# Two heads per store, computed side by side in TensorE's column halves, in a batched q·kᵀ kernel

## The chip, the cores and the metric

The kernel runs on one core of a Trainium2 chip. The metric is the device time of one execution in microseconds (us). The time before the change is the median of three runs, 1060.26 us (1059.48 to 1061.41).

## The reference

For 8 batches of 12 heads, so 96 heads, q and k are 1024 x 64 in float32 and the output is their product for every head, 1024 x 1024 in float32. Nothing is scaled and there is no softmax.

```python
batch, n_heads, seq, head_dim = 8, 12, 1024, 64

def reference(q, k):
    return np.einsum('bhid,bhjd->bhij', q, k).astype(np.float32)
```

The inputs are 50.3 MB, the output 402.7 MB.

## The kernel before

**Blocks.** The 96 heads are cut into blocks of 2, 2, 4, 8 and then 16 heads (`sizes`). q and k of a block are loaded, cast to float16 and transposed, so that the 64 elements of a head lie on partitions and the rows of a head along the free dimension. A block keeps half of its heads on partitions 0 to 63 and the other half on 64 to 127. Two sets of transposed buffers (`qk_sb`) alternate, so the next block is prepared while the present one is multiplied.

**How a block is prepared.** From block 3 on, q and then k of each block are loaded into the same tile `x_sb` (`Block.load`). Each load first waits on its issuing engine, ScalarE (ACT), until the last cast that reads `x_sb` is done (`input_busy`, set in `cast_quads`). GpSimd (POOL) casts a chunk in four instructions, one for each 32 partitions, into one of three `half` tiles (`cast_quads`, L220). VectorE (DVE) transposes the chunk in 32 x 32 squares into `qk_sb` (`transpose_quads`, L239), which frees the `half` tile. A block of 16 heads has 8 chunks of 2048 elements per partition, four for q and four for k. `TURNS` says after the first PSUM region of which head of the present block each of the next block's chunks is put into VectorE's queue. `LOADS` says after which region of which head ScalarE issues the next load. `to_half` puts casts into GpSimd's queue as early as the `half` tiles and the loads allow.

**The multiplication.** `scores` computes one head. PSUM is cut into two regions of 128 x 2048. For each of the four regions of a head, TensorE loads 128 columns of q (64 rows deep) and multiplies them with two stretches of 512 columns of k, twice. ScalarE copies the region to the output tile (L297), and TensorE goes on to the region after next when the copy is done. VectorE copies none of it, except in the first head. A head's output tile is 128 partitions x 8192 float32 values, 32 KB per partition, and there are three such tiles (`o_sb`, a `Ring`). The first copy of a head waits for the store that last read its tile.

**The stores.** When the copies of a head are done, SyncE (SP) issues one store of 4 MB: partition p holds rows 8p to 8p+7 of the head, one run of 32 KB both in the tile and in memory. The last head is split (`scores_split`) so that one of the 16 DMA engines, the one with partitions 16 to 19 and 48 to 51 (`APART`), is spared the rows of one half store.

**Queues.** Loads from block 4 on are issued from ScalarE's queue, in order with its copies. Stores and the first loads are issued from SyncE's queue. Every engine works in the order in which the Python code records its instructions. An instruction that waits holds all those behind it on its engine.

The lines of the wait before a load and of the wait before a copy are these:

```python
eng.wait(events)                       # Block.load: events = input_busy, the last cast out of x_sb
dma = eng.eng.dma_start(out=self.raw[x], in_=src.rearrange("(p r) d -> p (r d)", p=P))

copied = copier.run(lambda: ..., out_free + [done])   # scores: out_free = the store that last read the tile
```

Of the kernel before, what the change touches and what calls it, by code (L numbers as in the profile page):

```python
# [9 lines left out]
P = 128  # L10
# [53 lines left out]
def kernel(  # L64
# [10 lines left out]
    BH = B * H  # L75
    assert D == 64 and NT == 8 and BH >= 32 and BH % 16 == 0

    flat = [x.rearrange("b h s d -> (b h s) d") for x in (q, k)]
    of = out.rearrange("b h i j -> (b h) i j")

    sizes = [2, 2, 4, 8] + [16] * ((BH - 16) // 16)
    PE_BLOCKS, EARLY = 2, 3
    NMAX = max(sizes)
    CHUNK, HALVES = 64 * 32, 3
    TURNS = (3, 4, 5, 6, 10, 11, 12, 13)
    APART = (16, 48)
    LOADS = {0: {}, 1: {}, 2: {1: 3}, 3: {2: 1}}

# [5 lines left out]
    x_sb = pool.tile([P, NMAX * S * D // P], F32, name="x_sb", tag="x")  # L94
    half_sb = [pool.tile([P, CHUNK], F16, name=f"half{i}", tag=f"half{i}") for i in range(HALVES)]
    qk_sb = [
        [pool.tile([P, NMAX * S // 2], F16, name=f"{'qk'[x]}T{i}") for x in range(2)]
        for i in range(2)
    ]
    o_sb = [pool.tile([P, NT, S], F32, name=f"o_sb{i}", tag=f"out{i}") for i in range(3)]  # L100
    rest_q = pool.tile([P, 64], F16, name="rest_q", tag="rest_q")
# [38 lines left out]
    input_busy = []  # L140
    outs = Ring(o_sb)
    input_landing = [Landing(nc, f"x{i}_in") for i in range(2)]
    tail_landing = Landing(nc, "tail_out")
    rest_landing = Landing(nc, "rest_out")
    store_landing = {id(t): Landing(nc, f"out{i}_out") for i, t in enumerate(o_sb)}

    class Block:
        def __init__(self, i, first, N):
            self.i, self.first, self.N = i, first, N
            self.by_pe = i < PE_BLOCKS  # L150
            self.R = N * S // P
            self.elems = self.R * D
            self.cut = max(1, -(-self.R * 32 // CHUNK))
            self.raw = [None] * 2
            self.landed = [[] for _ in range(2)]
            self.rows = [None] * 2
            self.halves = {}
            self.qk = qk_sb[i % 2]
            self.ready = []
            self.over = []  # L160
# [104 lines left out]
        def scores(self, n, side, regions, w):  # L265
# [48 lines left out]
            out_busy.append(store_landing[id(buf)].start(dma))  # L314

        def scores_split(self, n, regions, w):
            half, g = divmod(n, self.N // 2)
# [138 lines left out]

    early, _, early_busy = outs.next()
    raw = early.rearrange("p t j -> p (t j)")
    at = 0
# [17 lines left out]
    def next_load(eng):  # L477
        if stream:
            b, x = stream.pop(0)
            earlier = (b.i, 0) if x else (b.i - 1, 1)  # L480
            assert b.i == EARLY or not any((i, c[0]) == earlier for i, c in casts)
            b.load(x, eng)
# [32 lines left out]
    def transposed(b, s):  # L515
        b.transpose_quads(*s)
        to_half(b.i)

    def block(i, heads, regions, w):
        b = blocks[i]  # L520
        nxt = blocks[i + 1] if i + 1 < len(blocks) else None
        for n in heads:
            side = {}
            if nxt and nxt.by_pe:
# [9 lines left out]
            elif nxt:  # L534
                parts = nxt.chunks()
                at = TURNS if i > EARLY else [m * b.N // len(parts) for m in range(len(parts))]
                some = [s for m, s in zip(at, parts) if m == n]
                side = {0: [lambda s=s: transposed(nxt, s) for s in some]}
            at = LOADS.get(i, {1: 1, 7: 1})
            if n in at:  # L540
                side[at[n]] = side.get(at[n], []) + [lambda: next_load(act)]
            if i == len(blocks) - 1 and n == b.N - 1:
                b.scores_split(n, regions, w)
            else:
                b.scores(n, side, regions, w)
            to_half(i + 2 + (n == b.N - 1))

# [49 lines left out]
```

## Time and profile before

The profiled execution took 1060.67 us, of which 1058.9 are the span of the profile.

| what | value |
|---|---|
| median of three runs | 1060.26 us (1059.48 to 1061.41) |
| profiled execution, its span | 1060.67 us, 1058.9 us |
| bytes read and written | 50.33 MB and 402.78 MB, 428 GB/s over the span |
| busy, share of the span: TensorE, ScalarE, VectorE, GpSimd | 66%, 66%, 41%, 34% |
| stores of 4 MB (L310) | 95 |
| loads of 4 MB from ScalarE's queue | 10 |

How to read it: the page gives for each engine its busy time, and for the 16 DMA engines the mean share of time in which they had a packet, in 40 slices of 26.5 us. A row of the groups gives the line of the kernel, engine, operation, output and input tiles with partitions x elements, how many there were, busy time, the mean duration of one in nanoseconds, and the idle time of the engine before them with what ended most of it. A packet in the DMA records is one row of a transfer here, that is what one partition holds.

### The profile page before, as it was taken

The page shows a single profiled execution, that of the slowest core. Times are in us where ns is not written, and L with a number is a line of the kernel's source. Part 1 is how long each engine was busy: PE and PEld are TensorE (multiplying, and loading weights), DVE is VectorE, ACT ScalarE, POOL GpSimd, SP SyncE. Part 2 cuts the span into 40 slices and gives each one's busy share as a digit, 9 for nine tenths or more (in the row PEclk, how much of TensorE's full clock was granted, in tenths as well). Part 3 has the DMA queues.
Part 4 walks back from the last instruction along what each step waited for, and adds up shares of the span by engine and source line. Part 5 has one row for each costly group of instructions (what it writes and reads, how often), then busy time and mean ns, then how long its engine had stood idle before and what let it go on. Part 6 is the DMA issues. An engine that isn't in the chain of part 4 may idle for free.

```text
span 1058.9 us, 3350 instructions
## 1 busy us (share of the span) xinstructions
PE 702.3 (66%) x1572; PEld 127.4 (12%) x802; DVE 435.4 (41%) x57; ACT 695.6 (66%) x385; POOL 358.3 (34%) x223
## 2 busy tenths in 40 slices
PE   6875754857477747657765756775674777787771
PEld 1111100111011101101110111110110111111110
DVE  2995939029194008539002917600580930000001
ACT  4766755857477748567765856775674777777771
POOL 7926555056280019065005609100822900000000
DMA  9999999999999999999999999999999999999998
GB/s 378 434 424 433 435 431 434 420 423 428 434 431 433 436 417 435 432 433 433 435 418 436 436 427 430 433 436 429 430 428 428 436 434 434 432 429 433 434 431 366
DMA packets 17186, 453.21 MB, mean 428 GB/s; under 512 B 1929, under 2 KB 1929, under 8 KB 2953
## 3 DMA queue, kind: packets, MB, share of 16 engines
q1 hardware_dynamic: 15008, 408.03, 89.5%
q10 hardware_dynamic: 2016, 42.99, 9.8%
q0 software_dynamic: 144, 1.97, 0.4%
q8 instruction: 9, 0.15, 0.0%
q14 instruction: 9, 0.07, 0.0%
HBM read 50.33 MB, written 402.78 MB: 428 GB/s over the span
## 4 chain that ended last, share of the span: by engine, by line
DMA 65%; ACT 15%; PE 8%; DVE 6%; POOL 4%; issue 1%; SPq 0%; ACTq 0%
DMA out_dram<-o_sb 60%; ACT o_sb L297 15%; PE ps_all L439 7%; DVE kT L239 4%; POOL half L220 3%; DMA x_sb<-in_q_dram 2%; DMA x_sb<-in_k_dram 2%; DVE qT L239 1%; DMA o_sb<-in_q_dram 0%; DVE x_sb L345 0%; DVE o_sb L345 0%; PE ps_all L253 0%; POOL qT L191 0%; DVE kT L260 0%; ACT kT L260 0%
## 5 line engine op out<-in xcount | busy, mean ns | idle before, releaser
L439 PE MATMUL ps_all<-kT,qT 64*128 64x512 f16 x1536 | 696.4, 617 | 327.1 <-ACT o_sb L297 310.0
L297 ACT COPY o_sb<-ps_all 128x2048 f32<-128x2048 f32 (+1 forms) x380 | 687.7, 1859 | 331.6 <-DMA out_dram<-o_sb 286.3
L220 POOL CAST half<-x_sb 32x2048 f16<-32x2048 f32 x176 | 332.5, 1889 | 482.7 <-DMA x_sb<-in_q_dram 307.9
L239 DVE STREAM_TRANSPOSE qT<-half 128x2048 f16<-128x2048 f16 x22 | 202.5, 9477 | 274.0 <-POOL half L220 274.0
L239 DVE STREAM_TRANSPOSE kT<-half 128x2048 f16<-128x2048 f16 x22 | 202.4, 9536 | 132.6 <-POOL half L220 132.6
L436 PEld LDWEIGHTS <-qT 64*128 64x128 f16 x768 | 124.0, 162 | 896.3 <-issue 875.9
L345 DVE COPY x_sb<-ps_all 128x2048 f32<-128x2048 f32 x1 | 2.3, 2292 | 174.0 <-PE ps_all L439 174.0
L374 POOL DMA_INDIRECT out_dram<-x_sb,place x1 | 1.2, 1157 | 176.6 <-DVE x_sb L345 176.6
L239 DVE STREAM_TRANSPOSE kT<-kT 128x1024 f16<-128x1024 f16 x2 | 9.3, 4856 | 0.0
L239 DVE STREAM_TRANSPOSE qT<-qT 128x1024 f16<-128x1024 f16 x2 | 9.2, 4782 | 0.0
L220 POOL CAST qT<-o_sb 32x1024 f16<-32x1024 f32 x8 | 8.3, 1036 | 1.1 <-DMA o_sb<-in_q_dram 0.7
L220 POOL CAST kT<-o_sb 32x1024 f16<-32x1024 f32 x8 | 8.3, 1036 | 0.5
L260 DVE COPY qT<-ps_all 128x1024 f16<-128x1024 f16 x2 | 2.4, 1224 | 11.4 <-PE ps_all L253 11.4
L253 PE MATMUL ps_all<-ident,qT 128*128 128x128 f16 x16 | 2.1, 311 | 7.1 <-POOL qT L191 7.0
L297 DVE COPY o_sb<-ps_all 128x1024 f32<-128x1024 f32 x4 | 4.9, 1225 | 4.4 <-PE ps_all L439 4.4
L345 ACT COPY x_sb<-ps_all 128x2048 f32<-128x2048 f32 (+1 forms) x2 | 3.7, 1860 | 2.1 <-PE ps_all L439 2.1
L260 ACT COPY kT<-ps_all 128x1024 f16<-128x1024 f16 x1 | 1.0, 1013 | 5.1 <-PE ps_all L253 5.1
L366 POOL COPY rest_q<-qT 64x8 f16<-64x8 f16 x4 | 0.6, 197 | 9.9 <-DVE kT L239 9.9
L345 DVE COPY o_sb<-ps_all 128x2048 f32<-128x2048 f32 x1 | 2.3, 2292 | 3.7 <-PE ps_all L439 3.7
L191 POOL CAST qT<-o_sb 128x512 f16<-128x512 f32 x4 | 2.3, 614 | 4.0 <-DMA o_sb<-in_q_dram 4.0
L260 ACT ACT_TABLE_LOAD x1 | 1.3, 1283 | 2.8 <-issue 2.8
L260 DVE COPY kT<-ps_all 128x1024 f16<-128x1024 f16 x1 | 1.2, 1225 | 4.4 <-PE ps_all L253 4.4
(18 smaller groups left out, 14.5 us busy)
## 6 DMA issues: line engine op xcount, KB each, us to landing
out_dram<-o_sb SPq DMA_DIRECT2D x95, 4096.0 KB, 21.8
x_sb<-in_q_dram ACTq DMA_DIRECT2D x5, 4096.0 KB, 25.2
x_sb<-in_k_dram ACTq DMA_DIRECT2D x5, 4096.0 KB, 23.4
x_sb<-in_q_dram SPq DMA_DIRECT2D x1, 2048.0 KB, 14.5
x_sb<-in_k_dram SPq DMA_DIRECT2D x1, 2048.0 KB, 18.9
out_dram<-o_sb SPq DMA_DIRECT2D x1, 2048.0 KB, 17.4
o_sb<-in_k_dram ACTq DMA_DIRECT2D x4, 256.0 KB, 5.2
o_sb<-in_q_dram SPq DMA_DIRECT2D x4, 256.0 KB, 5.4
```

The source lines that it names most:

```text
L191: lambda: nc.gpsimd.tensor_copy(out=rows[:, :, h], in_=self.raw[x][:, h * n : (h + 1) * n].rearrange("p (r d) -> p r d", d=D),),
L220: lambda: nc.gpsimd.tensor_copy(out=dst[q0 : q0 + 32].rearrange("p (r d) -> p r d", d=32), in_=raw[32 * b : 32 * b + 32, c * m : (c + 1) * ...
L239: lambda: nc.vector.transpose(out=dst, in_=buf.rearrange("p (r i) -> p r i", i=32)),
L253: lambda: nc.tensor.transpose(t_ps[:, t], rows[:, t], ident),
L260: lambda: copy(out=dst, in_=t_ps.rearrange("c t m -> c m t")), [done]
L297: lambda: (nc.vector.tensor_copy if by_dve else nc.scalar.copy)(out=dst, in_=ps[:, : w * S]),
L345: lambda: (nc.vector.tensor_copy if copier is dve else nc.scalar.copy)(out=dst[:, t * S : (t + w) * S], in_=ps[:parts, : w * S]),
L366: lambda: nc.gpsimd.tensor_copy(out=packed[:, t, 0, :, c], in_=rows[:, t, :, c]),
L374: nc.gpsimd.indirect_dma_start(out=out.rearrange("b h (m t) j -> (b h m) (t j)", t=T), out_offset=bass.IndirectOffsetOnAxis(ap=place_sb, a ...
L436: return nc.tensor.ldweights(stationary, tile_position=(at, to))
L439: return nc.tensor.add_instruction(mybir.InstMatmult(name=nc.get_next_instruction_name(), ins=[nc.tensor.lower_ap(moving), nc.tensor.lower ...
```

## The change

From head 8 on, two neighbouring heads are computed together (`scores_pair`) and stored with one store of 8 MB. Partition p holds rows 16p to 16p+15 of the two heads taken as one list of 2048 rows, so partitions 0 to 63 hold the first head and 64 to 127 the second, and a partition's run is 64 KB. For that, each of TensorE's instructions takes 64 columns of q instead of 128, and the two heads' instructions alternate: the first head's go to the array's columns 0 to 63 and the second's to columns 64 to 127. A region of PSUM now takes four weight loads and eight matmuls of 64 x 64 x 512 instead of two and four of 64 x 128 x 512, and a pair of heads has eight regions.

The output tiles are one tile of four 32 KB slots. Heads 0 to 7 and the last two use slots singly, the pairs use two neighbouring slots, so there are two pair buffers. To make room, blocks have 2, 2, 4, 6, 10 and then 12 heads, so `x_sb`, the `half` tiles and the transposed tiles are smaller. A load of a block of 12 has 24 KB per partition (3 MB). Chunks are 24 x 32, 20 x 32 and 32 x 32 elements per partition, 12 for a block of 12 heads and 16 for the block of 10.

In a pair VectorE copies regions 3 and 6 and ScalarE the other six; `HELP` lists the pairs in which VectorE takes only region 3, or none. `TURNS` now names head and region after which a chunk's transpose is put into VectorE's queue, `LOADS` the same for the loads in ScalarE's.

```diff
--- before.py
+++ after.py
@@ -73,18 +73,33 @@
     B, H, S, D = q.shape
     NT = S // P
     BH = B * H
-    assert D == 64 and NT == 8 and BH >= 32 and BH % 16 == 0
+    assert D == 64 and NT == 8 and BH >= 36 and BH % 12 == 0
 
     flat = [x.rearrange("b h s d -> (b h s) d") for x in (q, k)]
     of = out.rearrange("b h i j -> (b h) i j")
 
-    sizes = [2, 2, 4, 8] + [16] * ((BH - 16) // 16)
+    sizes = [2, 2, 4, 6, 10] + [12] * (BH // 12 - 2)
     PE_BLOCKS, EARLY = 2, 3
     NMAX = max(sizes)
-    CHUNK, HALVES = 64 * 32, 3
-    TURNS = (3, 4, 5, 6, 10, 11, 12, 13)
+    ROWS, HALVES = 32, 3
     APART = (16, 48)
-    LOADS = {0: {}, 1: {}, 2: {1: 3}, 3: {2: 1}}
+    PAIRS = 3
+    TURNS = {
+        1: [(n, 0) for n in range(2) for _ in range(2)],
+        2: [(n, 0) for n in range(4) for _ in range(2)],
+        3: [(0, 0)] * 8 + [(2, 7)] * 8,
+        4: [(0, 7)] * 2 + [(2, 4)] + [(2, 7)] * 3 + [(6, 7)] * 2 + [(8, 4)] + [(8, 7)] * 3,
+        5: [(0, 7)] * 2 + [(2, 4)] + [(2, 7)] * 3 + [(6, 7)] * 2 + [(8, 4)] + [(8, 7)] * 3,
+    }
+    LOADS = {
+        0: [],
+        1: [],
+        2: [(2, 3)],
+        3: [(2, 0), (4, 7)],
+        4: [(4, 0), (8, 7)],
+        5: [(4, 0), (10, 1)],
+    }
+    HELP = {3: {0: (), 2: (), 4: ()}, 4: {2: (3,), 8: (3,)}, 5: {2: (3,), 8: (3,)}}
 
     pool = ctx.enter_context(tc.tile_pool(name="sb", bufs=1))
     psum = ctx.enter_context(
@@ -92,12 +107,14 @@
     )
     ident = pool.tile([P, P], F16, tag="ident")
     x_sb = pool.tile([P, NMAX * S * D // P], F32, name="x_sb", tag="x")
-    half_sb = [pool.tile([P, CHUNK], F16, name=f"half{i}", tag=f"half{i}") for i in range(HALVES)]
+    half_sb = [pool.tile([P, ROWS * 32], F16, name=f"half{i}", tag=f"half{i}") for i in range(HALVES)]
     qk_sb = [
         [pool.tile([P, NMAX * S // 2], F16, name=f"{'qk'[x]}T{i}") for x in range(2)]
         for i in range(2)
     ]
-    o_sb = [pool.tile([P, NT, S], F32, name=f"o_sb{i}", tag=f"out{i}") for i in range(3)]
+    o_sb = pool.tile([P, 4 * NT, S], F32, name="o_sb", tag="out")
+    slots = [o_sb[:, i * NT : (i + 1) * NT] for i in (2, 3, 0, 1)]
+    doubles = [o_sb[:, 2 * NT :], o_sb[:, : 2 * NT]]
     rest_q = pool.tile([P, 64], F16, name="rest_q", tag="rest_q")
     place_sb = pool.tile([P, 1], I32, name="place", tag="place")
     place_f = pool.tile([P, 1], F32, name="place_f", tag="place_f")
@@ -138,11 +155,12 @@
         ]
     )
     input_busy = []
-    outs = Ring(o_sb)
+    outs = Ring(slots)
+    pairs = Ring(doubles)
     input_landing = [Landing(nc, f"x{i}_in") for i in range(2)]
     tail_landing = Landing(nc, "tail_out")
     rest_landing = Landing(nc, "rest_out")
-    store_landing = {id(t): Landing(nc, f"out{i}_out") for i, t in enumerate(o_sb)}
+    store_landing = {id(t): Landing(nc, f"out{i}_out") for i, t in enumerate(slots + doubles)}
 
     class Block:
         def __init__(self, i, first, N):
@@ -150,7 +168,7 @@
             self.by_pe = i < PE_BLOCKS
             self.R = N * S // P
             self.elems = self.R * D
-            self.cut = max(1, -(-self.R * 32 // CHUNK))
+            self.cut = next(c for c in range(1, self.R) if self.R % c == 0 and self.R // c <= ROWS)
             self.raw = [None] * 2
             self.landed = [[] for _ in range(2)]
             self.rows = [None] * 2
@@ -313,6 +331,62 @@
             )
             out_busy.append(store_landing[id(buf)].start(dma))
 
+        def scores_pair(self, n, side, regions, w, help):
+            qT = self.qk[0].rearrange("c (g m t) -> c g t m", t=2 * NT, m=D)
+            kT = self.qk[1].rearrange("c (g j) -> c g j", j=S)
+            where = [divmod(n + k, self.N // 2) for k in range(2)]
+            buf, out_free, out_busy = pairs.next()
+            written = {}
+            for u in range(2 * NT // w):
+                ps, ps_free, ps_busy = regions.next()
+                for tt in range(w):
+                    stationary = [
+                        qT[half * D : (half + 1) * D, g, w * u + tt] for half, g in where
+                    ]
+                    for k, (half, g) in enumerate(where):
+                        pe.run(
+                            lambda: load_weights(stationary[k], half * D, k * D),
+                            self.ready if n == 0 and u == 0 else [],
+                            signal=False,
+                        )
+                    for j in range(2):
+                        at = tt * S + j * 512
+                        for k, (half, g) in enumerate(where):
+                            moving = kT[half * D : (half + 1) * D, g, j * 512 : (j + 1) * 512]
+                            done = pe.run(
+                                lambda: multiply(
+                                    ps[k * D : (k + 1) * D, at : at + 512],
+                                    stationary[k],
+                                    moving,
+                                    half * D,
+                                    k * D,
+                                ),
+                                ps_free,
+                                signal=tt == w - 1 and j == 1 and k == 1,
+                            )
+                dst = buf[:, w * u : w * u + w].rearrange("p t j -> p (t j)")
+                copier = dve if u in help else act
+                copied = copier.run(
+                    lambda: (nc.vector.tensor_copy if u in help else nc.scalar.copy)(
+                        out=dst, in_=ps
+                    ),
+                    out_free + [done],
+                )
+                written[copier] = copied
+                ps_busy.append(copied)
+                for do in side.get(u, []):
+                    do()
+            self.over = [done]
+            sp.wait(written.values())
+            first = self.first + n
+            dma = nc.sync.dma_start(
+                out=of[first : first + 2]
+                .rearrange("h i j -> (h i) j")
+                .rearrange("(p t) j -> p (t j)", p=P),
+                in_=buf.rearrange("p t j -> p (t j)"),
+            )
+            out_busy.append(store_landing[id(buf)].start(dma))
+
         def scores_split(self, n, regions, w):
             half, g = divmod(n, self.N // 2)
             cs = slice(half * D, (half + 1) * D)
@@ -454,8 +528,8 @@
         blocks.append(Block(i, first, N))
         first += N
 
-    early, _, early_busy = outs.next()
-    raw = early.rearrange("p t j -> p (t j)")
+    early_busy = outs.busy[2]
+    raw = slots[2].rearrange("p t j -> p (t j)")
     at = 0
     for b in blocks[:EARLY]:
         for x in range(2):
@@ -519,7 +593,17 @@
     def block(i, heads, regions, w):
         b = blocks[i]
         nxt = blocks[i + 1] if i + 1 < len(blocks) else None
+        last = i == len(blocks) - 1
+        singles = range(b.N - 2, b.N) if last else range(b.N if i < PAIRS else 0)
+        at = lambda table: table.get(i, table[max(table)])
         for n in heads:
+            if n % 2 and n not in singles:
+                continue
+            if (i, n) == (PAIRS, 0):
+                pairs.busy = [outs.busy[m] + outs.busy[m + 1] for m in (0, 2)]
+            if last and n == b.N - 2:
+                outs.bufs, outs.n = slots[2:], 0
+                outs.busy = [list(pairs.busy[1]) for _ in range(2)]
             side = {}
             if nxt and nxt.by_pe:
                 if n == 1:
@@ -532,18 +616,19 @@
                         for u in (1, 3)
                     }
             elif nxt:
-                parts = nxt.chunks()
-                at = TURNS if i > EARLY else [m * b.N // len(parts) for m in range(len(parts))]
-                some = [s for m, s in zip(at, parts) if m == n]
-                side = {0: [lambda s=s: transposed(nxt, s) for s in some]}
-            at = LOADS.get(i, {1: 1, 7: 1})
-            if n in at:
-                side[at[n]] = side.get(at[n], []) + [lambda: next_load(act)]
-            if i == len(blocks) - 1 and n == b.N - 1:
+                for (m, u), c in zip(at(TURNS), nxt.chunks(), strict=True):
+                    if m == n:
+                        side.setdefault(u, []).append(lambda c=c: transposed(nxt, c))
+            for m, u in at(LOADS):
+                if m == n:
+                    side.setdefault(u, []).append(lambda: (next_load(act), to_half(i + 2)))
+            if last and n == b.N - 1:
                 b.scores_split(n, regions, w)
+            elif n in singles:
+                b.scores(n, side, regions, w)
             else:
-                b.scores(n, side, regions, w)
-            to_half(i + 2 + (n == b.N - 1))
+                b.scores_pair(n, side, regions, w, at(HELP).get(n, (3, 6)))
+            to_half(i + 2 + (n >= b.N - 2))
 
     for b in blocks[:PE_BLOCKS]:
         for x in range(2):
```

## The prediction

> **What bounds the kernel now.** I read the page first (slices, groups, DMA issues), then the chain of waits, the waits by engine, and the packet records.
>
> ```profile
> span 1058.9 us, 3350 instructions
> ...
> DMA  9999999999999999999999999999999999999998
> ...
> L297 ACT COPY o_sb<-ps_all 128x2048 f32<-128x2048 f32 (+1 forms) x380 | 687.7, 1859 | 331.6 <-DMA out_dram<-o_sb 286.3
> L220 POOL CAST half<-x_sb 32x2048 f16<-32x2048 f32 x176 | 332.5, 1889 | 482.7 <-DMA x_sb<-in_q_dram 307.9
> ...
> L345 DVE COPY x_sb<-ps_all 128x2048 f32<-128x2048 f32 x1 | 2.3, 2292 | 174.0 <-PE ps_all L439 174.0
> ...
> L220 POOL CAST qT<-o_sb 32x1024 f16<-32x1024 f32 x8 | 8.3, 1036 | 1.1 <-DMA o_sb<-in_q_dram 0.7
> ...
> x_sb<-in_q_dram ACTq DMA_DIRECT2D x5, 4096.0 KB, 25.2
> x_sb<-in_k_dram ACTq DMA_DIRECT2D x5, 4096.0 KB, 23.4
> ```
>
> The DMA engines never rest: from the first rows to the last few us all 16 have a packet. ScalarE waits 286.3 us for stores to free tiles; no engine but DMA is on the path after the start. So the time is bytes over rate plus any gap in the DMA queue, and each edit is judged by two questions: does it change the rate, and does it open a gap?
>
> The packet records give the rate. A row of 16,384 B takes 611 ns, one of 32,768 B 1,213 ns, so a row costs about 9 ns besides its bytes. Start to start on one engine it is 1,209 ns against 1,204.6 by the slope, so at least 4.6 ns. Stretches without loads run at 433.1 GB/s. The load stretches lose 4.3 us in all, which I leave as it is.
>
> The chain of waits shows what a gap would come from:
>
> ```profile
> 63.83 24.64 DMA x_sb<-in_q_dram
> ...
> 119.69 23.23 DMA x_sb<-in_k_dram
> ```
>
> A load takes 24 us though its own bytes are 9.7 us of DMA time. In the records the first row of the q load starts 3.84 us after its issue (1.0 to reach the engines, as for the kernel's first load, then up to three store rows already taken in), and then its rows start 2.42 us apart on each engine: one load row, one store row. Near the end 16 KB rows start 1.82 us apart beside 32 KB stores, so they alternate row for row whatever their size. In this kernel that is hidden: q and k of a block need 2 x (24 + 16 x 1.95 casts) = 110 us and a block of 16 heads lasts 175.
>
> **The change, part by part.**
>
> *Rows.* 43 pair stores replace 86 stores. Per engine 43 x 8 rows and 43 completions go: 43 x (8 x 4.6 + 6 ns) = 1.8 us, or 43 x 9 x 9 = 3.5 us by the longer reading. Four more loads take back 0.2. I take -1.6.
>
> *TensorE.* Eight matmuls in a row took 3.63 us, so 0.43 each. Two column halves at once are nowhere in this trace. Bounds: at once, a region stays at 4 x 0.43 + 0.2 = 1.9 us; one after the other it is 3.6 us. I take the first, since nothing couples the halves but the order of issue. A pair then takes eight regions at 1.95, 15.7 us from its first copy, plus 0.57 (last packet of the freeing store to the copy) and 1.0 (issue to first row): 17.3 of the 19.4 us of the other pair's store. That hides it with 2 us to spare, where three single tiles had about 10. The Trainium skill (TensorE: Matmul & The Clock Gate, Measured speedup vs the span model) gives 2.38x for three column tiles, 0.79 of ideal; an estimate from it is 2.2 us a region, which makes a pair 17.5 us instead of 15.7, and the sum about 5 us more.
>
> *ScalarE and VectorE.* Six copies of 1.87 and two of 2.29 per pair fit. But VectorE's copies now stand in its queue behind transposes, which wait for casts, which wait for loads. Behind the copy stand the region's release, ScalarE's next copies and the store.
>
> *Loads.* Beside 64 KB rows (2.41 us) a 24 KB row (0.91) takes 3.32, so a load takes 1.0 + 3 x 2.41 + 8 x 3.32 + 0.6 = 35 us when stores are queued. Casts of a q or k of 12 heads: 24 x (1.036 + 0.06) = 26.3; of 10 heads: 32 of 640 elements x 0.78 = 24.9 (0.83 ns per element and 0.18, from the two cast rows). Load and casts cannot overlap, since each load waits for the last cast out of the one `x_sb`. Per block 2 x (35 + 26.3) = 123 us against a block of 6 x 19.4 + 2 x 7.2 = 131. It fits, but hardly, and in the short blocks the chain starts behind:
>
> - q of block 4 is issued after head 6's last copy (71.8), lands at 92.9 (8 x 1.97 beside 32 KB rows), casts to 117.6.
> - k of block 4 then goes; ScalarE has stood at it since about 106, holding the second pair. That pair is stored at 131.2, the DMA queue (8.4 MB pair and 2.6 MB load) ends about 130. **Gap A: 1.0.**
> - k casts to 155.8; q of block 5 lands when the store of heads 12 and 13 is through, 178.4. Heads 14 and 15 follow to 197.9.
> - Heads 16 and 17: region 3 is VectorE's, behind two transposes of q of block 5. Landing 178.4 + 0.6 + first chunk's casts 4.4 + two transposes 8.9 = 192.3; copy 2.3, next region 1.9, three ScalarE copies 5.7: issued at 202.2, rows from 203.2. **Gap B: 5.3.**
> - q of block 5 is cast by 205.3, k lands 35 later, is cast at 267.4, q of block 6 lands at 295.8 behind the store of heads 22 and 23; heads 24 and 25 go out until 315.3. Heads 26 and 27 wait in the same way: 295.8 + 0.6 + 4.4 + 8.9 + 9.9 + 1.0 = 320.6. **Gap C: 5.3.**
> - From block 7 on q is issued at its place in ScalarE's queue (head 10, region 1), about 35 us before it is needed: no gap, no slack.
>
> *Skew.* One engine is slower: the last stores land every 9.76 us (ScalarE goes on at 1002.53, 1012.29, 1022.04), the mean rate makes 9.69. The end spares that engine eight rows of 16 KB, 4.9 us. With 2 us to spare in place of 10 the other 15 cannot run ahead; they idle some 3.6 us and end last, where before the slow one ended about 1.6 after them. I take +2 (bounds 0 and 4).
>
> Sum: -1.6 + 1.0 + 5.3 + 5.3 + 2 = +12.0, on the profiled execution's own 1060.67 (1.8 around its span) 1072.7. The median lies 0.4 lower, so I say **1072** (own range 1066 to 1079: each gap may be 2 us off, skew 2).
>
> **Rivals.**
>
> *Loads come in time (other side).* If beside 64 KB rows a load gets through by bytes or several rows at a turn, q of block 5 lands by 173 and q of block 6 by 290; that is the point from which gaps B and C are gone. Then the rows' saving is left: 1060.3 - 1.6 = 1058.7, at 3.5 saved 1056.8; about 1058. For it: nothing here shows 64 KB rows. Against: row for row at 32 and 16 KB. The Trainium skill (DMA: Bandwidth & Descriptors, Queues, rings and completion order) says that an engine drains a whole packet, typically 9 to 17 descriptors, from one ring before it turns to the next; by that the eight rows of a load would pass together, and this would be the result. The trace shows one row at a turn. Chance 0.27.
>
> *Every block late.* If a load is 3 us longer than 35 (a fourth row taken in ahead, 2.4, or weight loads that show), each of the last four blocks loses up to that: 4 x 2 to 3 more, 1080 to 1084. Chance 0.10.
>
> *It doesn't do what it says: 64 KB is moved as two rows of 32 KB.* The saving shrinks to 0.3, but loads take 1.0 + 3.6 + 8 x 2.12 + 0.6 = 22 to 24 us, gap C goes: 1060.3 - 0.3 + 1 + 5 + 2 = 1068. Chance 0.06.
>
> *TensorE becomes the bound.* Halves one after the other: 8 x 3.6 = 28.9 us a pair against 19.4, 43 x 9.5 = 409 less what loads cover and what the gaps were, 12 x 7.2 and 12: about 1060 + 310 at most, some 1310 where the start hides part. For it: only that no row shows them at once. Chance 0.05.
>
> **How the numbers follow.** Forecast 0.52, rivals 0.27, 0.10, 0.06, 0.05. What can be told from no change is 0.2%, 2.1 us: 1058.1 to 1062.4. The first rival splits on it, 0.18 faster (more than 2.1 saved, between the two readings of the rows) and 0.09 within; the forecast with its gaps nearly filled adds 0.02 within. Faster 0.18, same 0.11, slower 0.71. The range takes in the first rival and the forecast's upper edge: 1057 to 1081 leaves out TensorE, the worst of the late blocks and the best of the first rival, together under 0.2.
>
> **What would show it.** Right: DMA slices below 9 or a dip in GB/s to about 350 near 188 to 214 and 295 to 320; 24 KB loads landing 34 to 36 us after issue; VectorE's copies waiting behind transposes that GpSimd releases; store rows of 64 KB at about 2,417 ns; regions at 1.9 us. Wrong: loads of 24 us with no dip (first rival), rows of 1,213 ns in the pair stores (third), TensorE near 100% (fourth), dips once per block to the end (second). The forecast fails first if the q loads land earlier than I count, for 5 us early removes a gap whole.

## The result, and the profile after

The changed kernel takes 1092.57 us (median of 4 runs, 1091.73 to 1093.83), the kernel before 1060.38 beside it: a ratio of 1.0304, interval 1.0286 to 1.0322. It is slower, as forecast, but by 32 us where 12 were forecast. The span of the profiled execution is 1092.0 us. These are the page's lines of the changed kernel: the span, the 40 slices, two groups of copies, and the loads.

```profile
span 1092.0 us, 5673 instructions
...
PEclk9999655655555555555555555555555555555555
DMA  9999998899979999999999999999999999999998
GB/s 384 441 415 441 428 425 349 374 432 423 420 310 422 431 434 440 423 422 423 404 441 401 443 425 412 429 402 434 432 398 440 405 431 404 389 421 422 437 442 353
...
L370 ACT COPY o_sb<-ps_all 128x2048 f32<-128x2048 f32 x278 | 512.2, 1868 | 457.2 <-PE ps_all L513 246.6
...
L370 DVE COPY o_sb<-ps_all 128x2048 f32<-128x2048 f32 x66 | 154.4, 2340 | 346.5 <-PE ps_all L513 346.5
...
x_sb<-in_q_dram ACTq DMA_DIRECT2D x6, 3072.0 KB, 30.7
x_sb<-in_k_dram ACTq DMA_DIRECT2D x6, 3072.0 KB, 31.8
```

Three things are to be seen. The DMA row has slices of 8 and 7 where it had none but the last. The rate has its deep dips there (349, 374, 310), but it also dips to about 400 once or twice per block to the end, in slices whose DMA digit is 9. And ScalarE, whose longest wait was 286.3 us for stores before, now waits 246.6 us for TensorE, and still 201.6 us for stores.

A DMA digit of 9 says only that packets were under way, so I split the loss by the packet records of the two profiled executions. *Idle* is the time in which fewer than 16 packets were under way, each missing one counted as a sixteenth. *Longer packets* is what the rows took over the median of rows of their size (32 KB 1213 ns, 64 KB 2418, 24 KB 912), summed and divided by 16 engines.

| us | before | after |
|---|---|---|
| longer packets | 5.8 | 14.7 |
| all packets' time, per engine | 1057.2 | 1063.5 |
| idle at 176.4 to 181.8 | 0 | 4.7 |
| idle at 201.1 to 204.5 | 0 | 3.2 |
| idle at 297.2 to 300.3 | 0 | 2.6 |
| idle at 319.6 to 325.7 | 0 | 5.9 |
| idle from block 6 on, eight stretches up to 861 | 0 | 4.4 |
| idle at 908 to 953, the end of block 9 and what follows | 0 | 4.9 |
| idle at the very end | 1.9 | 1.4 |

Packets +6.3 and idle +25.2 make 31.5 of the 33.0 us between the last packets of the two kernels. Packets took 6.3 more although 64 KB rows are nominally shorter than two of 32 KB (2418 against 2426 ns, 2.8 us in all): the excess grew by 8.9.

The dips at 201 and 320 are the two that the prediction described. This is part of the chain of waits of the changed kernel (start us, duration us, what), from the landing of q of block 5:

```profile
160.36 18.62 DMA x_sb<-in_q_dram
178.97 0.05 issue
179.03 1.03 POOL half L238
...
183.37 4.41 DVE qT L257
187.78 0.49 issue
188.27 5.52 DVE qT L257
193.78 2.12 DVE o_sb L370
```

The load lands, GpSimd casts a chunk, VectorE transposes two chunks, and only then copies region 3 of heads 16 and 17. ScalarE waits 7.28 us before its next copy, and the store comes late.

The dips at 176.4 and 297.2 begin at the start of a block. This is ScalarE's timeline in the changed kernel (start, duration, what, and in brackets the idle time before with its releaser):

```profile
115.44 0.33 ACTq L189 DMA_DIRECT2D x_sb<-in_k_dram  x1
115.82 3.63 ACT L370 COPY o_sb<-ps_all 128x2048 f32<-128x2048 f32 x2 [8.04 <-POOL half L238]
...
160.36 0.33 ACTq L189 DMA_DIRECT2D x_sb<-in_q_dram  x1
165.28 3.63 ACT L370 COPY o_sb<-ps_all 128x2048 f32<-128x2048 f32 x2 [20.84 <-PE ps_all L513]
...
283.81 3.63 ACT L370 COPY o_sb<-ps_all 128x2048 f32<-128x2048 f32 x2 [14.98 <-PE ps_all L513]
```

At 165.28 and 283.81 the first pairs of blocks 4 and 5 begin. TensorE had waited for the last transposes of k: 20.7 us ahead of the one, 14.9 ahead of the other. A pair here takes 15.5 us from its first copy to the end of its last, and the rows of its store start about 1 us later, at 181.7 and 300.2. The queue had run dry at 176.4 and 297.2. In block 4 VectorE copies nothing ahead of these transposes. In block 5 it does, as its timeline shows:

```profile
244.56 10.40 DVE L257 STREAM_TRANSPOSE kT<-half 128x1024 f16<-128x1024 f16 x2
258.89 2.29 DVE L370 COPY o_sb<-ps_all 128x2048 f32<-128x2048 f32 x1 [3.93 <-PE ps_all L513]
261.10 20.64 DVE L257 STREAM_TRANSPOSE kT<-half 128x1024 f16<-128x1024 f16 x4
```

The last four transposes stand behind a copy that waits for TensorE. So this dip belongs to VectorE's copies as well, which e12 bears out.

### The profile page after: what moved, and what is told of

Read it like the earlier page. It is cut to its first block, busy times and chain, and to the rows that moved or that the text cites. A ratio compares the mean times of both kernels' runs of the same rounds, so it can differ in the third digit from the quotient of the medians.

```text
span 1092.0 us, 5673 instructions
## 1 busy us (share of the span) xinstructions
PE 694.1 (64%) x2948; PEld 166.3 (15%) x1490; DVE 626.2 (57%) x175; ACT 582.3 (53%) x319; POOL 395.6 (36%) x431
## 4 chain that ended last, share of the span: by engine, by line
DMA 41%; DVE 27%; PE 11%; ACT 8%; POOL 5%; issue 4%; SPq 0%; ACTq 0%
DMA out_dram<-o_sb 33%; DVE qT L257 13%; PE ps_all L513 11%; DVE kT L257 9%; ACT o_sb L370 7%; DMA x_sb<-in_q_dram 6%; POOL half L238 5%; DVE o_sb L370 5%; ACT o_sb L315 2%; DMA x_sb<-in_k_dram 2%; DMA o_sb<-in_q_dram 0%; DVE x_sb L419 0%; DVE o_sb L419 0%; PE ps_all L271 0%; POOL qT L209 0%
## 5 line engine op out<-in xcount | busy, mean ns | idle before, releaser
L513 PE MATMUL ps_all<-kT,qT 64*64 64x512 f16 (+1 forms) x2912 | 688.1, 612 | 365.6 <-ACT o_sb L370 238.3
L370 ACT COPY o_sb<-ps_all 128x2048 f32<-128x2048 f32 x278 | 512.2, 1868 | 457.2 <-PE ps_all L513 246.6
L238 POOL CAST half<-x_sb 32x1024 f16<-32x1024 f32 (+2 forms) x384 | 369.8, 963 | 532.7 <-DMA x_sb<-in_k_dram 220.6
L370 DVE COPY o_sb<-ps_all 128x2048 f32<-128x2048 f32 x66 | 154.4, 2340 | 346.5 <-PE ps_all L513 346.5
L510 PEld LDWEIGHTS <-qT 64*64 64x64 f16 (+1 forms) x1456 | 162.9, 212 | 887.6 <-issue 842.2
L257 DVE STREAM_TRANSPOSE qT<-half 128x1024 f16<-128x1024 f16 (+2 forms) x48 | 224.3, 4901 | 30.8 <-POOL half L238 30.7
L257 DVE STREAM_TRANSPOSE kT<-half 128x1024 f16<-128x1024 f16 (+2 forms) x48 | 224.2, 4906 | 21.9 <-POOL half L238 21.9
L315 ACT COPY o_sb<-ps_all 128x2048 f32<-128x2048 f32 (+1 forms) x36 | 62.2, 1773 | 18.0 <-PE ps_all L513 14.2
L419 DVE COPY o_sb<-ps_all 128x2048 f32<-128x2048 f32 x1 | 2.3, 2292 | 3.7 <-PE ps_all L513 3.7
(20 smaller groups left out, 16.4 us busy)
## 6 DMA issues: line engine op xcount, KB each, us to landing
out_dram<-o_sb SPq DMA_DIRECT2D x9, 4096.0 KB, 15.5
x_sb<-in_q_dram ACTq DMA_DIRECT2D x6, 3072.0 KB, 30.7
x_sb<-in_k_dram ACTq DMA_DIRECT2D x6, 3072.0 KB, 31.8
x_sb<-in_k_dram SPq DMA_DIRECT2D x1, 1536.0 KB, 16.4
```

Source lines behind the costliest of these rows:

```text
L238: lambda: nc.gpsimd.tensor_copy(out=dst[q0 : q0 + 32].rearrange("p (r d) -> p r d", d=32), in_=raw[32 * b : 32 * b + 32, c * m : (c + 1) * ...
L257: lambda: nc.vector.transpose(out=dst, in_=buf.rearrange("p (r i) -> p r i", i=32)),
L315: lambda: (nc.vector.tensor_copy if by_dve else nc.scalar.copy)(out=dst, in_=ps[:, : w * S]),
L370: lambda: (nc.vector.tensor_copy if u in help else nc.scalar.copy)(out=dst, in_=ps),
L419: lambda: (nc.vector.tensor_copy if copier is dve else nc.scalar.copy)(out=dst[:, t * S : (t + w) * S], in_=ps[:parts, : w * S]),
L510: return nc.tensor.ldweights(stationary, tile_position=(at, to))
```

## The experiments

Each line of the table gives the median of the timed runs and the split as above (stretches under 0.1 us left out). The last column is the ratio to the kernel before on the same chip, with its interval.

| kernel | us | longer packets | idle before 400 | idle from 400 on | idle at the end | ratio |
|---|---|---|---|---|---|---|
| changed | 1092.6 | 14.7 | 16.4 | 9.3 | 1.4 | 1.0304 (1.0286 to 1.0322) |
| e12: no copies by VectorE in blocks 4, 5 | 1084.1 | 16.3 | 5.9 | 9.3 | 1.6 | 1.0221 (1.0199 to 1.0243) |
| e1: none at all | 1076.9 | 18.7 | 2.3 | 2.1 | 3.7 | 1.0154 (1.0131 to 1.0178) |
| e5: e1 with 32 KB rows | 1069.4 | 11.6 | 2.5 | 0.3 | 1.0 | 1.0083 (1.0066 to 1.0100) |
| e9: e5, halves stored at once | 1062.6 | 6.4 | 0 | 0.1 | 1.4 | 1.0021 (1.0011 to 1.0031) |
| e4: heads singly, blocks of 12 | 1061.6 | 6.6 | 0 | 0 | 2.6 | 1.0007 (0.9997 to 1.0017) |
| before | 1060.4 | 5.8 | 0 | 0 | 1.9 | |

From the changed kernel over e12, e1, e5 and e9 to the kernel before, the steps are 8.5, 7.2, 7.5, 6.7 and 2.3 us. They add up to the whole 32.2 us, as steps from one end to the other must; what each step shows is in its section. The split is that of one profiled execution each.

### e1: no copies by VectorE

```diff
-    HELP = {3: {0: (), 2: (), 4: ()}, 4: {2: (3,), 8: (3,)}, 5: {2: (3,), 8: (3,)}}
+    HELP = {3: {}}
...
-                b.scores_pair(n, side, regions, w, at(HELP).get(n, (3, 6)))
+                b.scores_pair(n, side, regions, w, at(HELP).get(n, ()))
```

> Edit: ScalarE copies all eight regions of every pair, VectorE none; all else as in the changed kernel (1092.6). Theory (VectorE's copies stand behind transposes in its queue, so late or slow transposes hold back a store): without copies in that queue the dips at 180 to 220 and 300 to 340 and the one that recurs twice per block go, and ScalarE's eight copies of 1.87 fit in 19.4 us: 1060 (1058 to 1065). Rival 1 (two pair buffers leave too little time whoever copies): nothing is gained, 1088 or more. Rival 2 (the chain of load, cast and transpose of a 12-head block is itself longer than the block): TensorE waits at block starts in place of VectorE's copies, 1075 to 1090.

1076.9: half of what the theory promised. The page of this kernel, slices:

```profile
DMA  9999999999999999999999999999999999999998
GB/s 385 431 437 438 415 453 403 422 400 428 431 430 395 442 394 446 408 440 427 401 424 438 417 429 407 447 404 418 429 417 437 415 414 430 432 427 434 427 437 356
```

All deep dips are gone, idle time fell from 27.1 to 8.1 us, and the kernel still loses 16.5 us on the kernel before: the rate falls to about 400 wherever a load runs. So VectorE's copies were one cause, worth 15.7 us. Of the rest, 10.2 us are time in packets (1067.4 per engine against 1057.2), which is no wait of an engine, and 6.2 are idle time. Rival 1 falls as it was put (nothing gained); the time left over is of the kind that it named, and e5 to e11 take it apart. The time lies in the range of rival 2 (1075 to 1090), but its mechanism does not show: TensorE's waits for k's transposes at block starts fell from 38.6 to 31.2 us in all, and in e4 they are 37.8 us and cost nothing.

### e2: the sixth transpose later

```diff
-        5: [(0, 7)] * 2 + [(2, 4)] + [(2, 7)] * 3 + [(6, 7)] * 2 + [(8, 4)] + [(8, 7)] * 3,
+        5: [(0, 7)] * 2 + [(2, 4)] + [(2, 7)] * 2 + [(4, 7)] + [(6, 7)] * 2 + [(8, 4)] + [(8, 7)] * 2 + [(10, 4)],
```

> Edit: in blocks of 12 the sixth transpose of q is recorded after region 7 of the next pair, the sixth of k after region 4 of the next pair, so no more than three transposes stand between two copies of VectorE. Theory: three of 5.2 us and the copy are 18 us, under the 19.4 of a pair, so the dip that recurs twice per block from 440 on goes (about 1.4 us each, eleven of them, 15 us) and the two early dips stay: 1077 (1073 to 1081). Rival 1 (two pair buffers too tight): 1090 or more. Rival 2 (chain longer than the block): 1090 or more, with the last transpose later still.

1090.6 (1088.1 to 1091.3): a miss, 2.0 us gained where 15 were expected, at the time that both rivals gave. I had taken the recurring dips in GB/s for idle time of 1.4 us each. Most of that was longer packets. As e1 had gained 15.7 us with the same two buffers, and e4 shows the chain of the blocks to be short enough, neither rival explains it as put. Four transposes in a row do hold a copy back, as VectorE's timeline of the changed kernel shows at the end of block 9:

```profile
919.18 2.29 DVE L370 COPY o_sb<-ps_all 128x2048 f32<-128x2048 f32 x1 [1.67 <-PE ps_all L513]
921.39 20.66 DVE L257 STREAM_TRANSPOSE kT<-half 128x1024 f16<-128x1024 f16 x4
941.61 2.56 DVE L370 COPY o_sb<-ps_all 128x2048 f32<-128x2048 f32 x1
```

From copy to copy it is 22.4 us, and a pair has 19.4. Here no load follows any more, and it costs 3.0 us of idle time at 949.4. In the blocks before, the same three lines stand beside a load whose rows (7.3 us of DMA time) fill the queue meanwhile. In e2 the idle time at 908 to 953 shrinks from 4.9 to 0.4, the dips before block 6 stay (16.5).

### e3: the output step of the transposes

```diff
+            if self.N == 12:
+                at, side = divmod(part * self.cut + c, 2)
+                dst = self.qk[x][:, at * 2048 : (at + 1) * 2048].rearrange(
+                    "c (i r) -> c r i", i=32
+                )[:, side * m : (side + 1) * m]
...
```

> Edit: the transposes of the 12-head blocks write with a step of 64 elements between a square's columns in place of 96, each chunk to its own place; the output is wrong for these heads, the amount of work is the same. Theory (the price of a transpose follows the step): one takes 4.4 to 4.8 us in place of 5.45, four in a row 18 in place of 20.7, so most of the recurring dip goes: 1078 (1074 to 1083). Rival 3 (VectorE is slowed by GpSimd's casts beside it, not by the step): 5.4 us each and 1092 as before.

1088.0, a miss. Transposes of 1024 elements, in the changed kernel (step 96):

```profile
L257 DVE STREAM_TRANSPOSE kT<-half 128x1024 f16<-128x1024 f16 x36 | 186.3, 5458 | 0.0
```

and in e3 (step 64):

```profile
L263 DVE STREAM_TRANSPOSE kT<-half 128x1024 f16<-128x1024 f16 x36 | 167.5, 4958 | 0.0
```

So the step alone, with the same casts beside it, moves the price by 0.50 us, 9%, and rival 3 falls. In the kernel before (step 128) 2048 elements took 9.5 us, 4.75 for 1024. The time followed by less than expected, 4.6 us, which fits what e2 showed: four in a row are late mostly where a load covers it.

### e4: heads singly

```diff
-    PAIRS = 3
+    PAIRS = 99
...
+                    if m + u // 4 == n:
+                        side.setdefault(u % 4, []).append(lambda c=c: transposed(nxt, c))
...
```

> Edit: every head stored singly (32 KB per partition) from four slots, copied by ScalarE alone, with the blocks of 12, the chunks, the loads and the transposes where the changed kernel has them. Theory: the new blocks cost nothing by themselves, only the pairs with VectorE's copies do: 1061 (1059 to 1064). Rival 2 (the chain of a 12-head block is too long): 1072 or more, with TensorE waiting at block starts.

1061.6, the ratio 1.0007 (0.9997 to 1.0017) can't be told from 1. The blocks of 12, the smaller chunks, the slow transposes and four more loads cost nothing that shows, and the loads land in 22.0 us. TensorE waits 37.8 us for k's transposes at block starts, about as in the changed kernel, and between the start and the end the queue never runs dry. So all of the loss belongs to the pairs and the copies given to VectorE for them.

### e5 and e8: the same pairs in 32 KB rows

```diff
...
+            for h in range(2):
+                cols = slice(h * NT * S, (h + 1) * NT * S)
+                dma = nc.sync.dma_start(
+                    out=dst[:, cols], in_=buf.rearrange("p t j -> p (t j)")[:, cols]
+                )
+                out_busy.append(store_landing[id(buf)].start(dma))
```

> Edit on e1 (1076.9): each pair's store is issued as two stores behind each other, the first and the second 32 KB of every partition, both after the last copy, both into the same count. So the rows are 32 KB and the buffers, copies and waits are those of e1. In e1 the packets take 9.3 us more per DMA engine than with single stores, nearly all of it in 64 KB rows beside loads, and the engines idle 5.8 us more. Theory (64 KB rows beside loads are what costs): the excess falls from 14 to about 5 us, 1.6 come back for more rows: 1069 (1066 to 1072). Rival (the two pair buffers cost, by idle engines): 1074 or more.

1069.4, as expected: 7.5 us less than e1. The excess of the packets falls by 7.1, of which 2.8 are given back since two rows of 32 KB nominally take 8 ns more than one of 64, and idle time falls by 4.3. The loads in the DMA issues of e5 (KB each, median us from issue to landing):

```profile
x_sb<-in_q_dram ACTq DMA_DIRECT2D x6, 3072.0 KB, 21.9
x_sb<-in_k_dram ACTq DMA_DIRECT2D x6, 3072.0 KB, 23.0
```

> Edit on the changed kernel (1092.6): its pair stores as two stores of 32 KB rows, as in e5, VectorE's copies kept. Theory (loads are late since a load row waits for a whole 64 KB row, and then VectorE's copies behind the transposes hold stores back): loads land in 22 to 25 us in place of 31 to 35, the dips at 180 to 220 and 300 to 340 lose most of their 16 us, and 8 us of longer packets go: 1072 (1067 to 1078). Rival (the dips come from the two pair buffers and the copies alone): 1084 or more.

e8 makes the same edit on the changed kernel: 1080.6 (ratio 1.0193, 1.0176 to 1.0210). Its loads land in 21.9 and 23.0 us too. The dip at 320 is gone, 1.1, 5.9 and 2.5 us are left near 177, 200 and 298, and 2.4 near 937. So loads that come 9 us earlier remove one of the dips and not the others: at 200 VectorE's copy is still behind two transposes (they begin at 182.42, the copy at 192.41). Its 12 us are less than the theory's 20, more than the rival's 8.

### e6 and e7: loads in the stores' ring

```diff
-                    side.setdefault(u, []).append(lambda: (next_load(act), to_half(i + 2)))
+                    side.setdefault(u, []).append(lambda: (next_load(sp if i >= PAIRS else act), to_half(i + 2)))
```

> Edit on e1: from block 3 on the loads are issued from SyncE's queue, at the same place in the order of the code, so that they stand in the same ring as the stores and pass between two stores in place of row by row beside one. Theory A (the turn from one ring to the other is what lengthens the 64 KB rows): the excess falls from 14 us to 2 or less, loads land in about 28 us: 1066 (1062 to 1070). Theory B (reading beside writing costs, whatever the ring): the same excess, 1075 or more.

1084.5. Theory A falls. 64 KB rows lost most of their excess (14.4 to 6.2 us), but now the 24 KB rows of the loads, which all engines read at once, take 1036 ns in the mean instead of 947: 11.9 us of excess, 19.9 in all. The rows of a load now pass together (a load's rows all start within some 10 us, where e1 took 25), so the turns from ring to ring are gone, and yet a load costs about the same in either ring, as theory B has it. The slices of e6 show one dip more:

```profile
DMA  9999969999999999999999999999999999999998
GB/s 385 436 427 440 430 256 420 434 451 427 427 430 407 442 405 415 441 410 427 420 429 429 396 453 403 419 444 408 427 413 438 427 397 449 405 456 431 425 427 359
```

SyncE's timeline there:

```profile
120.68 0.33 SPq L382 DMA_DIRECT2D out_dram<-o_sb  x1
157.91 0.34 SPq L189 DMA_DIRECT2D x_sb<-in_q_dram  x1
158.30 20.00 SPq L382 DMA_DIRECT2D out_dram<-o_sb  x2
```

It stands at the load of q of block 5 until 157.9, for casts, with a finished pair's store behind it: 9.0 us idle, which is the edit's own fault and more than the 7.6 us by which it lost.

> Edit on the kernel before (1060.4): the loads of the blocks of 16 go from SyncE's queue, nothing else. Theory A: the 5.4 us by which its 32 KB rows are longer than their median fall to 1.5: 1056.5 (1055 to 1058). Theory B: 1060. Rival (SyncE stands at the load until the casts are done, and the stores behind it come late): 1063 or more.

In the kernel before the same move gives 1064.5 (1.0036, 1.0024 to 1.0049). Its longer packets are 6.5 us, no fewer than before, and the idle time at the end, when some engines are done before others, is 5.2 us instead of 1.9. Theory A falls here as well. The time is that of the rival (1063 or more). SyncE does stand 11.0 us at loads for casts, but between the start and the end the queue is idle for 0.2 us only, so no late store shows. Why the engines end further apart was not followed up.

### e9: each half stored when it is copied

```diff
...
+                if u % 4 == 0:
+                    buf, out_free, out_busy = outs.next()
+                    written = {}
...
+                if v == 3:
+                    sp.wait(written.values())
+                    dma = nc.sync.dma_start(
+                        out=rows[u // 4], in_=buf.rearrange("p t j -> p (t j)")
+                    )
+                    out_busy.append(store_landing[id(buf)].start(dma))
...
```

> Edit on e5 (1069.4): the pairs are computed as before in TensorE's column halves, but each half of a pair's rows (32 KB per partition, regions 0 to 3 and 4 to 7) takes one of four single buffers, waits only for that buffer's last store and is stored as soon as its four copies are done. Theory (what is left of the pairs' price, 7.8 us over single heads in e4, comes from two large buffers that are filled and freed as wholes): as e4, 1062 (1060 to 1065). Rival (the 64 KB pitch of the rows in memory, or the column halves, cost it): 1067 to 1070.

1062.6, as the theory has it, though 2.3 us over the kernel before, just clear of the noise. The slices of e9:

```profile
DMA  9999999999999999999999999999999999999998
GB/s 393 434 422 431 423 438 424 432 423 429 434 425 435 432 428 434 423 432 432 432 433 424 430 435 435 432 422 433 432 429 435 426 435 430 432 433 430 435 429 370
```

Nothing under 422 between the ends. TensorE's column halves, the 64 KB pitch in memory and the order of the instructions are those of the pairs, so what they cost is within the 1.0 us between e9 and e4. With four buffers of 32 KB the longer packets are 6.4 us where two buffers had 11.6 with rows of the same size. That second 5 us I can place (4.7 of it in rows beside loads) but not explain; the edit changes the number of buffers and the moment of the stores together.

### e10 and e11: without loads

```diff
-    stream = [(b, x) for b in blocks[EARLY:] for x in range(2)]
+    stream = [(b, x) for b in blocks[EARLY:7] for x in range(2)]
+    for b in blocks[7:]:
+        b.ready = blocks[b.i - 2].ready
...
```

> Edit on e1 (1076.9): from block 7 on nothing is loaded, cast or transposed; these blocks multiply what lies in the transposed tiles from two blocks before, and the output of their 48 heads is not the reference's. Eight loads of 3 MB go, 25.2 MB, 58 us at 433 GB/s. Theory (64 KB rows cost only beside loads, about 1.0 us more per load than single heads, and idle time follows from it): 1076.9 - 58 - 8 x 1.45 - 1.5 = 1006, about 5.5 over e11. Rival (pairs cost all along, two buffers being too few): 1013 or more, 12 or more over e11. By the prediction's row overhead of 4.6 ns the 24 pairs without loads would give back 0.9.

> Edit on e4 (1061.6): the same loads, casts and transposes left out as in e10, heads stored singly. 1061.6 - 58 - 8 x 0.4 = 1000.5 under both, the base for e10.

1008.9 and 1002.3: 6.6 us apart, where e1 and e4 are 15.3 apart. Taking eight of the loads away took 8.7 us of the pairs' price away, 1.1 per load, near the 1.0 expected; the rival's 12 is far. Between 540 and 960 us no load runs in either: 64 KB rows moved 430.5 GB/s, 32 KB rows 431.1. The stretch of 64 KB rows holds 1.6 us of idle time; without it the rate would be 432.1. So the larger rows by themselves are about 0.2% faster (2428 ns in the mean, against 2 x 1219), and the short gaps between pairs take back more than that. With the loads, their casts and transposes went too; that the price lay in the loads' bytes alone is not shown.

### e12: VectorE's copies left out in two blocks only

```diff
...
+        4: {n: () for n in range(10)},
+        5: {n: () for n in range(12)},
+        6: {2: (3,), 8: (3,)},
...
```

> Edit on the changed kernel (1092.6): VectorE copies nothing in the pairs of blocks 4 and 5 (heads 14 to 35), where the two large dips lie; from block 6 on it copies as before. Theory (both dips are VectorE's copies behind transposes that start late): 16 us of idle time go, 2 come back in longer packets, since loads meet more stores: 1078 (1075 to 1081), and the small idle stretches from block 6 on stay as they are, so that it ends 1 to 4 us over e1 (1076.9). Rival (the dips are the start of the chain falling behind, and move to block 6 when it is left more time): 1084 or more.

1084.1: 8.5 us gained instead of 14. The time is at the edge of the rival (1084 or more), but no dip moved to block 6. The dips at 201, 297 and 320 shrink from 11.7 to 0.9 (0.6 more at 381), packets take 1.6 back. That at 297 goes because block 5 begins 10 us earlier (283.81 in the changed kernel):

```profile
273.60 3.63 ACT L375 COPY o_sb<-ps_all 128x2048 f32<-128x2048 f32 x2 [7.72 <-PE ps_all L518]
```

The one at 176 stays at 4.5: it is the start of block 4 waiting for k, whoever copies. In e1, whose code is the same up to there, it was 1.2: there k landed 17.3 us after its issue instead of 20.5, and block 4 began 2.8 us earlier. From block 6 on idle time is 9.3 as in the changed kernel, and 7.2 us separate it from e1, not 1 to 4: VectorE's copies cost nearly as much in the steady blocks as in the two dips.

## Why the prediction had the direction right and the size wrong

**TensorE: right.** "At once, a region stays at 1.9 us": in the trace the matmuls of the two halves start within 0.01 us of each other (both at 700.18, for one), and a region takes 1.88 us in the chain. The Trainium skill's 0.79 of ideal for three column tiles (TensorE: Matmul & The Clock Gate, Measured speedup vs the span model) did not show with two halves: the 2.2 us a region that the prediction estimated from it did not come. The granted clock reads 0.56 where it read 1.0, and the pitch of the matmuls stayed at 0.43 us.

**Loads: right as a mechanism, nearly in size.** One load row, then one 64 KB row, on each engine; 30.7 and 31.8 us to landing, where 35 were forecast: I had counted a store row for each of the eight load rows, and only seven stand between them, 2.4 us less. In e6, in the stores' own ring, they took as long. The rule of the Trainium skill (DMA: Bandwidth & Descriptors, Queues, rings and completion order) that a whole packet of descriptors goes through at a turn was the rival with 0.27; the rows alternate one by one here too, and it did not come.

**Gaps B and C: right in place and cause.** Forecast at 197.9 and 315.3 with 5.3 us each; measured at 201.1 with 3.2 and at 319.6 with 5.9. Landing 178.97 (178.4 + 0.6 forecast), cast at 183.37 (183.4). The step "two transposes 8.9" was short: 10.4, of which the output step of 96 explains 1.0 (9.4 in e3). Gap B is smaller because the store ahead of it was late itself. That gap C came out near its size is partly luck: q of block 6 landed at 300.1 instead of 296.4 (295.8 + 0.6), and the store ahead ended 4.3 us late as well.

**Gap A and the block starts: wrong.** "Gap A: 1.0" at 130 did not come. The next line failed: "k casts to 155.8; ... Heads 14 and 15 follow to 197.9" treats the pair as ready. It cannot begin until k is also transposed. The casts ended at 160.3, since k landed at 135.6, the last transpose at 163.2, and the first copy came at 165.3. That is 4.7 us of idle time at 176.4. The 2.6 at 297.2 are of the same kind, with VectorE's copies holding up the last transposes (e12). I followed the loads and casts to their end and forgot that the first pair of a block waits for all of k. With four single buffers the same wait costs nothing (e4); it is the pair's longer way to its first store that lets the queue run dry.

**"From block 7 on ...: no gap, no slack": wrong.** It was 9.3 us from block 6 on. No slack means a gap wherever anything varies: VectorE's copy behind four transposes (22.4 us between two copies against a pair's 19.4), and perhaps engines that run apart. e12 and e1 put 7.2 us on VectorE's copies there. The skew, taken as +2, can't be told apart here from other small gaps. In e1 there are 2.1 us of small stretches and 1.9 more at the end than before, which would be the upper bound; in the changed kernel the end is 0.5 shorter than before.

**Rows, -1.6: the saving was there; that rows beside loads get longer was put at nothing.** By their medians the 64 KB rows are 2.8 us shorter in all, between the prediction's 1.8 and 3.5, and without loads (e10, e11) they are shorter too. But packets took 6.3 us more. The overhead per row was applied to stores that run beside 14 loads. "The load stretches lose 4.3 us in all, which I leave as it is" was the failing step: that loss is one of longer packets, 0.5 us per load before, 0.9 in the changed kernel and 1.2 in e1. It grows with the row (e5) and falls when each half is stored from one of four smaller buffers (e9). Why is open.

The prediction's sum, term by term (us):

| term | forecast | measured |
|---|---|---|
| rows (time in packets) | -1.6 | 6.3 |
| gap A, measured as the two block starts | 1.0 | 7.3 |
| gap B | 5.3 | 3.2 |
| gap C | 5.3 | 5.9 |
| skew, measured as idle from block 6 on and at the end | 2 | 8.8 |
| sum | 12.0 | 31.5 |

The rival "every block late" (1080 to 1084) named the sign of the steady loss but looked for it in longer loads, which were shorter than forecast. e8 tests the rival "two rows of 32 KB" (1068): its load time of 22 to 24 us and "gap C goes" came as worked out, and 1080.6 because the block starts and the copies from block 6 on were left out there too.

No kernel of these that does all the work beats the kernel before; e4 alone can't be told from it.

## What to carry to other kernels

Here, where the transfers never rested, the engines had nothing to win: count what a change does to slack and to the moment at which each buffer is freed, and leave copies out of a queue in which work from the input chain stands. Follow a staged chain to its last consumer (here TensorE's first use of k), not to its last producer. When a rate falls while the DMA share stays at 9, look at the durations of single packets before looking for a wait.

## What the runs showed of the hardware that was not expected

- Store rows beside loads last longer, the more so the larger: a 64 KB row of 2418 ns reached 3286 ns at its 99th percentile. In e1 they are for the most part the rows just ahead of a load's first row (11 of 16 engines at 452.9 to 453.0, 3.1 to 3.3 us). Moving the loads into the stores' ring moved much of the excess from the store rows to the load rows (e6). What sets it is open.
- A transpose of 1024 float16 elements per partition in 32 x 32 squares took 5.46 us at an output step of 96 elements, 4.96 at 64 and 4.75 at 128 (half of 9.5 us for 2048 in the kernel before). At 48 it was 4.0 us for 768 and at 80 2.9 us for 640, 5.3 and 4.6 when scaled to 1024. Steps of 48 and 96 are the slow ones among those seen.
- The profile's granted clock fell to 0.56 with the column halves in every kernel that used them and stayed at 1.0 in e4, without any change in the pace of the matmuls.
